# Rotary embedding kernel: half of unit 2 loaded as fp32 over ScalarE's queue, half of unit 3 stored by GpSimd

## Chip, cores and metric

One core of one Trainium2 chip. The metric is device microseconds of one execution; lower is better. "Span" is the time from the first to the last record of the profile. A DMA is one transfer between the chip's main memory (HBM) and the core's own (SBUF); a cast changes the number type, here between fp32 and fp16.

## The reference

The input `x` is (8, 8, 1024, 64) fp32, 16.8 MB, and the output is as large. For every position the two halves of the last dimension are rotated by an angle:

```python
angles = np.outer(positions * scale, freqs)          # (1024, 32)
cos, sin = np.cos(angles), np.sin(angles)
out_first  = x_first * cos - x_second * sin
out_second = x_first * sin + x_second * cos
```

## The kernel before

The 64 heads are cut in four "units" of 4 MB, each a tile of 128 partitions by N = 8192 elements (half: NH = 4096). GpSimd loads most of the data and lets the DMA cast it from fp32 to fp16; the second half of unit 0 alone comes as fp32 in two quarters over SyncE's and ScalarE's queues, and ScalarE casts it. VectorE rotates in fp16, ScalarE casts each half to fp32, and the result is stored. (`pin` keeps an instruction at its place in the program's order; lines are left out at `...` and at comments.)

```python
X0f = xout.tile([P, N], FP32, tag="O")               # staging, shares a slot with the outputs
Q = NH // 2
pin(nc.sync.dma_start(out=X0f[:, :Q], in_=xv[0][:, NH : NH + Q]))
pin(nc.scalar.dma_start(out=pos_i64, ...)); pin(nc.scalar.dma_start(out=freq_row, ...))
pin(nc.scalar.dma_start(out=X0f[:, Q:NH], in_=xv[0][:, NH + Q :]))
pin(nc.gpsimd.dma_start(out=Xf[0][:, :NH], in_=xv[0][:, :NH]))       # casts on the way
# ... small constants ...
for u in range(1, NU):
    c = C2 if u == NU - 1 else 0                     # unit 3 in two pieces
    pin(nc.gpsimd.dma_start(out=Xf[u][:, : N - c], in_=xv[u][:, : N - c]))
    if c:
        pin(nc.gpsimd.dma_start(out=Xf[u][:, N - c :], in_=xv[u][:, N - c :]))
# ... sine and cosine tables: VectorE, ScalarE, TensorE ...
pin(nc.scalar.copy(out=Xf[0][:, NH:], in_=X0f[:, :NH]))
for u in range(NU):
    OUT = xout.tile([P, N], FP32, tag="O")           # three slots
    for s in range(2):
        # ... pr = Xs*sin; Xs = Xs*cos; subtract; add (VectorE, fp16) ...
        pin(nc.scalar.copy(out=OUT[:, ns], in_=Xf[u][:, ns]))
        if u in (0, NU - 1):
            pin(nc.sync.dma_start(out=ov[u][:, ns], in_=OUT[:, ns]))
    if u not in (0, NU - 1):
        pin(nc.gpsimd.dma_start(out=ov[u], in_=OUT))
```

## Time and profile before

| | before |
|---|---|
| time, median of the 6 runs beside the change | 84.39 us |
| span of the profiled execution | 82.4 us |
| VectorE / ScalarE busy | 60.3 / 40.1 us |
| 16 DMA engines busy, three queues together | 80.2 us |
| first and last DMA packet | 1.75 and 81.15 us |
| last store landed | 81.5 us |

"Packet" is here one row of one partition, as the records of the trace have it; spread evenly, each of the 16 engines has 8 of the 128 rows of a DMA. The packets' times sum to more than the 79.4 us between first and last, as some packets of an engine overlap in the records: the sum measures work, not elapsed time. The first packet starts 1.75 us after the span's start and the last ends at 81.15; the DMA engines fill the time between.

### The profile page before, as it was taken

To read this page: it belongs to the slowest core of one execution; us is meant where nothing else is said; L and a number is where in the kernel's file an instruction comes from. 1 tells how busy PE (TensorE), PEld (TensorE's weight loads), DVE (VectorE), ACT (ScalarE), POOL (GpSimd) and SP (SyncE) were. 2 spreads that over 40 slices of the span, in tenths; PEclk is the share of its full clock that TensorE was granted. 3 is DMA by queue.
4 is the path that set the end of the run, shared out by engine and by line. 5 is a ranking of instruction groups with operands and counts; after the bars stand their busy time and mean duration, and the time that the engine had idled before them with its cause. 6 is when DMAs were issued, how large, how long until landed. Compare 5 with 4: busy or idle time off the path is not lost.

```text
span 82.4 us, 183 instructions
## 1 busy us (share of the span) xinstructions
PE 6.0 (7%) x18; PEld 2.4 (3%) x18; DVE 60.3 (73%) x40; ACT 40.1 (49%) x18; POOL 5.1 (6%) x15
## 2 busy tenths in 40 slices
PE   0011797100000000000000000000000000000000
PEld 0011232000000000000000000000000000000000
DVE  0306277999999999999999999999999998000000
ACT  0602259999950690294088049309705911950000
POOL 4950000000000000000000200000110000000000
PEclk9999999995555555555555555555555555555555
DMA  2899997996996999899899899997995998989992
GB/s 44 345 312 286 282 350 167 255 255 143 239 255 127 255 255 334 302 308 280 239 322 266 239 398 330 545 430 334 509 509 255 509 509 350 414 382 469 422 414 95
DMA packets 2018, 26.22 MB, mean 318 GB/s; under 512 B 354, under 2 KB 354, under 8 KB 482
## 3 DMA queue, kind: packets, MB, share of 16 engines
q0 software_dynamic: 1008, 15.73, 66.5%
q1 hardware_dynamic: 720, 9.44, 27.5%
q10 hardware_dynamic: 290, 1.06, 3.3%
HBM read 16.79 MB, written 16.78 MB: 407 GB/s over the span
## 4 chain that ended last, share of the span: by engine, by line
DVE 54%; ACT 15%; issue 7%; DMA 6%; PE 5%; DVEq 1%; ACTq 0%
DVE X L157 20%; DVE pr L156 20%; DVE X L161 9%; DMA freq_row<-in_freqs_dram 6%; ACT T L143 5%; DVE X L158 5%; ACT OUT L164 4%; ACT X L144 4%; PE ps L133 4%; DVEq L197 1%; PE cfreq L101 1%; ACT tab L126 1%; DVE r L117 1%; DVE y L108 1%; ACTq L70 0%
## 5 line engine op out<-in xcount | busy, mean ns | idle before, releaser
L164 ACT CAST OUT<-X 128x4096 f32<-128x4096 f16 x8 | 28.8, 3606 | 24.2 <-DVE X L161 24.2
L156 DVE TENSOR_TENSOR pr<-X,T 128x4096 f16<-128x4096 f16 x8 | 18.3, 2292 | 0.8 <-ACT T L143 0.5
L157 DVE TENSOR_TENSOR X<-X,T 128x4096 f16<-128x4096 f16 x8 | 18.3, 2292 | 0.3
L158 DVE TENSOR_TENSOR X<-X,pr 128x2048 f16<-128x2048 f16 x8 | 9.8, 1224 | 0.3
L161 DVE TENSOR_TENSOR X<-pr,X 128x2048 f16<-128x2048 f16 x8 | 9.7, 1217 | 0.0
L143 ACT CAST T<-ps 128x1024 f16<-128x1024 f32 x6 | 5.7, 1030 | 2.4 <-PE ps L133 2.4
L133 PE MATMUL ps<-tab,sel 128*128 128x512 f16 x16 | 5.4, 489 | 2.8 <-ACT tab L126 2.2
L168 POOL DMA_DIRECT2D out_dram<-OUT x2 | 1.1, 537 | 53.7 <-ACT OUT L164 53.7
L141 DVE CAST T<-ps 128x1024 f16<-128x1024 f32 x2 | 2.4, 1224 | 2.2 <-PE ps L133 2.2
L144 ACT CAST X<-X0f 128x4096 f16<-128x4096 f32 x1 | 3.6, 3650 | 0.0
L99 DVE COPY sel<-one 128x2048 f16<-128x2048 f16 x1 | 0.7, 693 | 2.8 <-POOL one L88 2.8
L121 ACT ACTIVATE tab<-r 128x256 f16<-128x256 f32 x1 | 0.4, 416 | 4.4 <-DVE r L117 4.4
L121 ACT ACT_TABLE_LOAD x1 | 1.3, 1283 | 2.1 <-issue 2.1
L133 PEld LDWEIGHTS <-sel 128*128 128x128 f16 x16 | 1.9, 120 | 5.9 <-issue 5.3
L94 POOL DMA_DIRECT2D X<-in_x_dram x3 | 2.0, 659 | 0.0
L104 DVE CAST posf<-pos_i 128x8 f32<-128x8 int32 x1 | 0.2, 171 | 2.1 <-DMA pos_i<-in_positions_dram 2.1
L101 PE MATMUL cfreq<-freq_row,coef 1*128 1x32 f32 x2 | 0.6, 392 | 5.9 <-DMA freq_row<-in_freqs_dram 5.9
L108 DVE TENSOR_TENSOR y<-posf,cfreq 128x256 f32<-128x256 f32 x1 | 0.4, 423 | 0.7 <-PE cfreq L101 0.7
L84 POOL DMA_DIRECT2D X<-in_x_dram x1 | 0.7, 667 | 0.8 <-POOLq L183 0.8
L101 PEld LDWEIGHTS cfreq<-freq_row,coef 1*128 1x128 f32 x2 | 0.5, 306 | 5.9 <-issue 5.9
L96 POOL DMA_DIRECT2D X<-in_x_dram x1 | 0.6, 558 | 0.0
L126 ACT ACTIVATE tab<-ra,quarter 128x256 f16<-128x256 f32 x1 | 0.5, 507 | 0.0
(11 smaller groups left out, 2.3 us busy)
## 6 DMA issues: line engine op xcount, KB each, us to landing
out_dram<-OUT SPq DMA_DIRECT2D x4, 2048.0 KB, 14.2
out_dram<-OUT POOLq DMA_DIRECT2D x2, 4096.0 KB, 14.8
X<-in_x_dram POOLq DMA_DIRECT2D x2, 2048.0 KB, 25.7
X<-in_x_dram POOLq DMA_DIRECT2D x1, 1792.0 KB, 44.6
X0f<-in_x_dram SPq DMA_DIRECT2D x1, 1024.0 KB, 4.7
X<-in_x_dram POOLq DMA_DIRECT2D x1, 1024.0 KB, 11.5
X0f<-in_x_dram ACTq DMA_DIRECT2D x1, 1024.0 KB, 13.4
X<-in_x_dram POOLq DMA_DIRECT2D x1, 256.0 KB, 47.7
```

Of the source, the lines that this page charges most:

```text
L94: pin(nc.gpsimd.dma_start(out=Xf[u][:, : N - c], in_=xv[u][:, : N - c]))
L101: nc.tensor.matmul(out=cfreq, lhsT=coef, rhs=freq_row, start=True, stop=True)
L121: pin(nc.scalar.activation(out=tab[:, 0], in_=r, func=AF.Sin, bias=0.0, scale=-_TWO_PI_DN))
L133: nc.tensor.matmul(out=ps[:, i].rearrange("p t w -> p (t w)"), lhsT=sel[:, g + i].rearrange("s h q -> s (h q)"), rhs=tab.rearrange("s t k ...
L141: pin(nc.vector.tensor_copy(out=dst, in_=ps))
L143: pin(nc.scalar.copy(out=dst, in_=ps))
L144: pin(nc.scalar.copy(out=Xf[0][:, NH:], in_=X0f[:, :NH]))
L156: pin(nc.vector.tensor_tensor(out=pr, in0=Xs, in1=sin_b, op=ALU.mult))
L157: pin(nc.vector.tensor_tensor(out=Xs, in0=Xs, in1=cos_b, op=ALU.mult))
L158: pin(nc.vector.tensor_tensor(out=Xs[:, :, 0, :], in0=Xs[:, :, 0, :], in1=pr[:, :, 1, :], op=ALU.subtract))
L161: pin(nc.vector.tensor_tensor(out=Xs[:, :, 1, :], in0=pr[:, :, 0, :], in1=Xs[:, :, 1, :], op=ALU.add))
L164: pin(nc.scalar.copy(out=OUT[:, ns], in_=Xf[u][:, ns]))
```

## The change

The intent, as far as the diff tells it: relieve GpSimd's queue of a sixth of its later loads (2 of 12 MB), use ScalarE's idle time for the cast, and let GpSimd share the last stores.

```diff
+    UF = 2
     pin(nc.scalar.dma_start(out=X0f[:, Q:NH], in_=xv[0][:, NH + Q :]))
+    pin(nc.scalar.dma_start(out=X0f[:, NH:], in_=xv[UF][:, NH:]))
...
     for u in range(1, NU):
         c = C2 if u == NU - 1 else 0
+        if u == UF:
+            pin(nc.gpsimd.dma_start(out=Xf[u][:, :NH], in_=xv[u][:, :NH]))
+            continue
...
             pin(nc.scalar.copy(out=OUT[:, ns], in_=Xf[u][:, ns]))
+            if (u, s) == (0, 1):
+                pin(nc.scalar.copy(out=Xf[UF][:, NH:], in_=X0f[:, NH:]))
             if u in (0, NU - 1):
-                pin(nc.sync.dma_start(out=ov[u][:, ns], in_=OUT[:, ns]))
+                eng = nc.gpsimd if (u, s) == (NU - 1, 0) else nc.sync
+                pin(eng.dma_start(out=ov[u][:, ns], in_=OUT[:, ns]))
```

## The prediction

> **What bounds the kernel now.** I began with the page's busy shares, because they name the obvious suspect, and then its table of DMA queues.
>
> ```profile
> PE 6.0 (7%) x18; PEld 2.4 (3%) x18; DVE 60.3 (73%) x40; ACT 40.1 (49%) x18; POOL 5.1 (6%) x15
> q0 software_dynamic: 1008, 15.73, 66.5%
> q1 hardware_dynamic: 720, 9.44, 27.5%
> q10 hardware_dynamic: 290, 1.06, 3.3%
> HBM read 16.79 MB, written 16.78 MB: 407 GB/s over the span
> ```
>
> VectorE is busy for 73% of the span, but the three DMA queues together take 66.5 + 27.5 + 3.3 = 97.3% of the time of the 16 DMA engines, that is 80.2 of 82.4 us. q0 is GpSimd's queue, q1 SyncE's, q10 ScalarE's. (q0's 15.73 MB count the bytes written; its loads read fp32 and write fp16, so 7.34 MB of loads stand for 14.68 MB read, beside 8.39 MB of stores.) Next I asked for the DMA share in stretches that leave out the first 2 us, before the first packet, and the last, after it.
>
> ```profile
> 2.00:12.00 10.00, 3.86 (x11) 1.79 (x12) 4.03 (x8) 3.20 (x4) 3.12 (x8) 1.00 1.00 303
> 12.00:22.00 10.00, 2.16 (x9) 0.62 (x7) 9.31 (x6) 9.86 (x7) 0.00 (x0) 0.83 1.07 230
> 22.00:32.00 10.00, 0.00 (x0) 0.00 (x0) 9.86 (x6) 5.44 (x2) 0.00 (x0) 0.50 0.97 220
> 62.00:72.00 10.00, 0.00 (x0) 0.00 (x0) 7.54 (x5) 5.93 (x2) 0.00 (x0) 0.50 0.96 415
> 2.00:81.50 79.50, 6.02 (x18) 2.41 (x18) 60.30 (x40) 40.13 (x18) 4.20 (x10) 0.60 1.00 329
> ```
>
> The column before the last is the DMA share: 1.00 from 2.0 to 81.5 us. (Rows stray between 0.9 and 1.07 because a packet is credited where it starts. Cutting the packet records into 1 us bins, I find 1.00 to 1.07 of the engines busy in every bin between the first and the last.) The DMA engines never rest, so bytes set the end. The other candidate is VectorE and the tail behind it: half of the chain of waits (54%) is VectorE. From the timeline (start, duration), and the landing time of the store issued from 73 to 74 us:
>
> ```profile
> 13.19 2.29 DVE L156 TENSOR_TENSOR pr<-X,T 128x4096 f16<-128x4096 f16 x1 [0.47 <-ACT T L143]
> ...
> 27.39 2.29 DVE L156 TENSOR_TENSOR pr<-X,T 128x4096 f16<-128x4096 f16 x1
> 27.45 3.60 ACT L164 CAST OUT<-X 128x4096 f32<-128x4096 f16 x1 [3.61 <-DVE X L161]
> ...
> 69.67 3.60 ACT L164 CAST OUT<-X 128x4096 f32<-128x4096 f16 x1 [3.39 <-DVE X L161]
> ```
>
> ```profile
> out_dram<-OUT SPq DMA_DIRECT2D x1, 2048.0 KB, 8.2
> ```
>
> VectorE runs without a gap from 13.19 to 69.65 us. ScalarE's last cast ends at 73.27, and the last 2 MB store, issued there, lands 8.2 us later, at 81.5. By itself it would be faster: SyncE's first load started about 1.25 us after its issue, and 8 rows per engine of 16 KB at 0.611 us take 4.9 us, so VectorE's chain alone would let the end come at about 73.3 + 1.25 + 4.9 + 0.2 = 79.7. It lands at 81.5 because unit 2's store holds the engines until about 72 and the first half of unit 3 goes before it. VectorE thus has about 1.8 us to spare at the last store.
>
> **What the Trainium skill says.** "DMA: Bandwidth & Descriptors", section "Issuing engines are not separate DMA queues": transfers started by different engines run on the same 16 DMA engines and interleave. The 97.3% sum agrees. The same page, "Queues, rings and completion order", says that each engine takes turns among the queues by packet. The trace agrees: when GpSimd's load of unit 2 and SyncE's store of unit 0 overlap, 28 to 34 us, each queue passes 48 packets. The same page, "SWDGE vs HWDGE vs iDMA", says that only GpSimd's DMAs can cast, which is why the moved load needs a ScalarE cast. "ScalarE: Activation LUTs", section "What ACT_TABLE_LOAD costs", gives 186 ns + 0.833 ns per element with immediate operands: 3598 ns for 4096; the trace has 3606 and 3650.
>
> **The change part by part.**
>
> *The moved load.* 2 MB of unit 2 leave q0, where a row of 16 KB fp32 became 8 KB fp16, and enter q10, where it stays fp32. HBM bytes do not change. DMA time: in the packet records a cast packet from 16 KB takes 0.624 us and one from 32 KB 1.227 us; a plain packet of 16 KB takes 0.611 to 0.624 (stores) and one of 8 KB 0.307 to 0.322. That is 26.3 to 26.8 GB/s per engine in every kind. 128 packets times at most 0.013 us, over 16 engines, is 0.1 us. The cast in the DMA was free, so taking it out gains nothing.
>
> *The new cast.* One ScalarE cast of 128x4096 fp32 to fp16, 3.65 us as in this row:
>
> ```profile
> L164 ACT CAST OUT<-X 128x4096 f32<-128x4096 f16 x8 | 28.8, 3606 | 24.2 <-DVE X L161 24.2
> L144 ACT CAST X<-X0f 128x4096 f16<-128x4096 f32 x1 | 3.6, 3650 | 0.0
> ```
>
> It stands in order behind the OUT cast of unit 0's second half, which runs 27.45 to 31.05, so it runs 31.05 to 34.70. The next OUT cast started at 34.44: 0.26 us late, with 3.4 us of idle time behind it (the 24.2 us over seven waits). It delays no VectorE work.
>
> *Where the order of arrival moves.* This is the one sensitive spot. The moved load queues behind unit 0's quarter and starts at about 12.5, when unit 0's transfers end. From then q10 takes turns with q0's load of unit 1, which had the engines to itself and landed at 22.5 (issued about 2.7, 19.8 to land). Per engine there are 8 packets of 1.227 us and now 8 of about 0.62 between them: it lands about 8 x 0.62 = 5.0 us later, at about 27.5. VectorE wants unit 1 at 27.39. SyncE's store of unit 0, issued at 23.86, does not push it further: before, its first packet started at 28.7, about 1.25 us of issue and three packets already in the engines after its issue. So VectorE stalls by 0 to 0.6 us, I take 0.2. ScalarE gets its fp32 at about 28, before 31.05. Unit 2's first half then needs only 2 MB from q0 and lands near 37 (8 packets each of q0 and q1, 9.8 us after 27.5), wanted at 41.49; unit 3 lands near 51, wanted at 55.58. No other load is late.
>
> *The store.* Half 0 of unit 3 goes to q0, in line behind unit 2's 4 MB, instead of q1. Before, it was issued at 66.3 and its first packet came near 71, as unit 2's ended: it already ran where it would on q0. The other half, issued at 73.3, found it still running until 76.6. On two queues they might alternate, but the same 4 MB leave at the same rate, 16 x 0.611 = 9.8 us from 72. GpSimd's issue costs 0.54 us on an idle engine. Sum: 0.
>
> *Buffers.* The staging tile shares its slot with unit 2's output; ScalarE first writes that at 48.53, and the new reader ends at 34.70. No wait.
>
> Sum: the DMA work changes by at most 0.1 us and VectorE shifts by about 0.2, out of a slack of 1.8 us at the last store and of about 1 to 1.5 us at unit 2's store (issued 59.48, wanted by the engines at 62.1, less 1 to 1.5 us that a GpSimd DMA may take to start). I put 84.4 us.
>
> **Rivals.** *A late unit 1 is felt.* If the engines favour q10, or its load is served ahead of q0, unit 1 could land at 29 to 30, and VectorE stalls 2 to 2.5 us. Then unit 2's store starts late while nothing else is in any queue, the engines rest 1 to 1.5 us, and the end moves to 85.5 to 86. For it: the 27.5 against 27.39 has no margin. Against it: turns by packet gave equal counts in the trace, and q10's rows are half as long as q0's. *The cast in the DMA has a cost that I miss*, and moving it and spreading the last store speeds up the end. For it: that is the likely intent. Against it: packet times per byte are equal, and the engines have no idle time to win; 33.56 MB in the 79.4 us from first to last packet are already 423 GB/s, at 26.8 per engine the most would be 428, so at best 1.1 us: 83.3. *ScalarE becomes the bound.* It goes from 40.1 to 43.8 us of 82; the row above shows 3.4 us of idle before each cast, so no.
>
> **Range and chances.** Runs of one kernel spread by 0.3 us. The downside is the stall, the upside half a microsecond of better interleaving: 83.8 to 85.5. Faster by 2% would need 82.7, under what the bytes allow: 0.02. Slower by 2% needs 86.05, a stall near 3 us: 0.06. Same: 0.92.
>
> **What would show it.** The DMA share over 2 to 81.5 stays 1.00 and the three shares still sum to about 80 us. q10 grows by 2.1 MB to 3.2 and by about 5 us of engine time, 6% of the span, to 9.4%; q1 falls to 7.34 MB and 21.5%; q0 loses 1.05 MB of load and gains 2.10 of store, for 16.78 MB at an unchanged 66.5%. The row of the staging cast becomes x2 at about 3650 ns. The pr row of VectorE waits at most 0.6 us for unit 1's load. The last store still lands near 81.5. I am wrong if a wait of VectorE for that load exceeds 1.5 us and the engines show a gap after 62, or if a fp32 packet of 16 KB takes clearly other than 0.62 us.

## The result and the profile after

84.90 us median of 6 runs (84.72 to 85.11) beside 84.39 of before; ratio 1.0063, interval 1.0041 to 1.0085. Ratios here are the mean time of one kernel's runs over the mean of the other's of the same rounds, so they are not quite the ratio of the medians quoted. The change is "same" at 2%, and slower by a small amount that is clear of the noise. The page after has the busy shares and queues as foreseen:

```profile
PE 6.9 (8%) x18; PEld 2.7 (3%) x18; DVE 60.3 (73%) x40; ACT 43.7 (53%) x19; POOL 5.7 (7%) x16
q0 software_dynamic: 1152, 16.78, 65.8%
q1 hardware_dynamic: 576, 7.34, 21.5%
q10 hardware_dynamic: 434, 3.15, 9.9%
HBM read 16.79 MB, written 16.78 MB: 406 GB/s over the span
```

The queues now sum to 97.2% of 82.7 us, 80.4 us of engine time; the HBM bytes are the same to the last digit shown. In the stretches of the span the engines again rest nowhere (DMA share before the last column):

```profile
22.00:32.00 10.00, 0.00 (x0) 0.00 (x0) 9.11 (x6) 6.39 (x3) 0.00 (x0) 0.50 0.99 281
2.00:81.50 79.50, 6.95 (x18) 2.70 (x18) 60.31 (x40) 43.65 (x19) 4.74 (x11) 0.60 1.01 342
```

The timeline shows the one new wait of VectorE, and the new cast:

```profile
27.32 3.61 ACT L170 CAST OUT<-X 128x4096 f32<-128x4096 f16 x1 [3.61 <-DVE X L167]
28.02 2.29 DVE L162 TENSOR_TENSOR pr<-X,T 128x4096 f16<-128x4096 f16 x1 [0.79 <-DMA X<-in_x_dram]
...
30.83 3.60 ACT L172 CAST X<-X0f 128x4096 f16<-128x4096 f32 x1
...
35.07 3.61 ACT L170 CAST OUT<-X 128x4096 f32<-128x4096 f16 x1 [0.64 <-DVE X L167]
```

The page's rows of the two staging casts, and the landing of the last store (issued between 73 and 75 us):

```profile
L149 ACT CAST X<-X0f 128x4096 f16<-128x4096 f32 x1 | 3.6, 3648 | 0.0
L172 ACT CAST X<-X0f 128x4096 f16<-128x4096 f32 x1 | 3.6, 3599 | 0.0
```

```profile
out_dram<-OUT SPq DMA_DIRECT2D x1, 2048.0 KB, 7.8
```

The new cast is as long as the old one, and the last store, issued at 74.00, lands at 81.8: issued 0.7 us later than before, it lands only 0.3 later. VectorE waits 0.79 us for unit 1, which shared the engines with the moved load. Everything on VectorE is from there on some 0.7 us later, yet the last DMA packet ends at 81.42 instead of 81.15. ScalarE's cast fits in its gap: the next output cast starts when VectorE is ready.

A trap stands in the chain of waits: it now runs through this load,

```profile
DVE 45%; DMA 30%; issue 6%; ACT 4%; DVEq 1%; POOL 1%; POOLq 0%
```

and gives "DMA 30%" to it. One could read that the load of unit 1 has become the bound. The chain follows who released whom; it cannot see that the last store waited in the engines behind other stores, so its percentages do not say what a shorter wait is worth.

One more number comes from the list of runs: time minus span, per run. Before: 1.77 us (median of the 40 runs beside the experiments). After: 2.06 (median of 6). So of the 0.5 us, about 0.25 lie inside the span (median 82.6 against 82.85) and about 0.3 outside it, where the profile shows nothing.

### The profile page after: what moved, and what is told of

It is laid out like the page before. It is cut to its first block, busy times and chain, and to the rows that moved or that the text cites. A ratio compares the mean times of both kernels' runs of the same rounds, so it can differ in the third digit from the quotient of the medians.

```text
span 82.7 us, 186 instructions
## 1 busy us (share of the span) xinstructions
PE 6.9 (8%) x18; PEld 2.7 (3%) x18; DVE 60.3 (73%) x40; ACT 43.7 (53%) x19; POOL 5.7 (7%) x16
## 3 DMA queue, kind: packets, MB, share of 16 engines
q0 software_dynamic: 1152, 16.78, 65.8%
q1 hardware_dynamic: 576, 7.34, 21.5%
HBM read 16.79 MB, written 16.78 MB: 406 GB/s over the span
## 4 chain that ended last, share of the span: by engine, by line
DVE 45%; DMA 30%; issue 6%; ACT 4%; DVEq 1%; POOL 1%; POOLq 0%
DMA X<-in_x_dram 30%; DVE pr L162 17%; DVE X L163 17%; DVE X L167 7%; DVE X L164 5%; ACT OUT L170 4%; DVEq L206 1%; POOL one L90 0%; POOL coef L87 0%; POOL one L89 0%; POOL X L86 0%; DVEq L162 0%; POOL quarter L88 0%; POOLq L192 0%
## 5 line engine op out<-in xcount | busy, mean ns | idle before, releaser
L170 ACT CAST OUT<-X 128x4096 f32<-128x4096 f16 x8 | 28.9, 3607 | 21.5 <-DVE X L167 21.5
L138 PE MATMUL ps<-tab,sel 128*128 128x512 f16 x16 | 6.3, 582 | 2.2 <-ACT tab L131 2.2
L177 POOL DMA_DIRECT2D out_dram<-OUT x2 | 1.1, 538 | 54.4 <-ACT OUT L170 54.4
L149 ACT CAST X<-X0f 128x4096 f16<-128x4096 f32 x1 | 3.6, 3648 | 0.0
L172 ACT CAST X<-X0f 128x4096 f16<-128x4096 f32 x1 | 3.6, 3599 | 0.0
L99 POOL DMA_DIRECT2D X<-in_x_dram x2 | 1.4, 720 | 0.0
L175 POOL DMA_DIRECT2D out_dram<-OUT x1 | 0.5, 533 | 6.5 <-ACT OUT L170 6.5
L86 POOL DMA_DIRECT2D X<-in_x_dram x1 | 0.7, 669 | 0.8 <-POOLq L192 0.8
```

What stands on the lines that cost most here:

```text
L138: nc.tensor.matmul(out=ps[:, i].rearrange("p t w -> p (t w)"), lhsT=sel[:, g + i].rearrange("s h q -> s (h q)"), rhs=tab.rearrange("s t k ...
L172: pin(nc.scalar.copy(out=Xf[UF][:, NH:], in_=X0f[:, NH:]))
```

## Experiments

**The two parts alone, and the load elsewhere.** The edits, against the change (e1, e3, e4) or against before (e2):

```diff
# e1_load_only: the change without its store
-                eng = nc.gpsimd if (u, s) == (NU - 1, 0) else nc.sync
-                pin(eng.dma_start(out=ov[u][:, ns], in_=OUT[:, ns]))
+                pin(nc.sync.dma_start(out=ov[u][:, ns], in_=OUT[:, ns]))
# e2_store_only: before with the change's store
# e3_fp32_on_q0: e1, with the load on GpSimd's queue and the cast one step later
-    pin(nc.scalar.dma_start(out=X0f[:, NH:], in_=xv[UF][:, NH:]))
+            pin(nc.gpsimd.dma_start(out=X0f[:, NH:], in_=xv[UF][:, NH:]))   # behind unit 2's first half
-            if (u, s) == (0, 1):
+            if (u, s) == (1, 0):
# e4_load_late: e1, with the load still on ScalarE's queue, issued behind unit 0's cast; cast as in e3
```

> The load and its cast alone; the last stores as before. Theory 'load' (the fp32 load shares the engines with unit 1's load and its packets take longer: 0.24 us more engine time in the changed kernel): 84.8 to 84.9 us, with the 0.7 us wait of VectorE for unit 1. Rival 'store' (GpSimd's store costs the time): 84.4 us.

> The store on GpSimd's queue alone. Theory 'load': 84.4 us, engine time 80.1 us, last landing as before. Rival 'store': 84.9 us.

> Unit 2's second half still comes as fp32 and is cast by ScalarE (one step later), but over GpSimd's queue behind unit 2's first half, so that nothing is added beside unit 1's load; stores as before. If fp32 against cast in the DMA matters by itself: 84.7 to 84.9, or under 84.2 if the cast had a cost. If only the place in the order matters: 84.4 us, no wait of VectorE for unit 1.

> The fp32 load stays on ScalarE's queue, but is issued behind the cast of unit 0's quarters (about 20 us), so that it meets unit 2's first half and SyncE's store and not unit 1. Unit 1 lands by 24, VectorE waits for nothing. If VectorE's 0.7 us wait is what the 0.5 us are: 84.4. If the meeting of three queues lengthens packets whatever they carry: 84.7 to 84.9 without any wait.

| | DMAs (on SyncE's and ScalarE's queues) | time us | ratio to before | span us | time minus span | VectorE's wait for unit 1 |
|---|---|---|---|---|---|---|
| before | 15 (8) | 84.39 | | 82.6 | 1.77 | none |
| after | 16 (8) | 84.90 | 1.0063 | 82.85 | 2.06 | 0.8 |
| e1 load only | 16 (9) | 85.26 | 1.0105 | 83.2 | 2.06 | 0.5 |
| e2 store only | 15 (7) | 84.37 | 1.0001 | 82.6 | 1.77 | none |
| e3 fp32 on q0 | 16 (8) | 84.81 | 1.0048 | 82.75 | 2.04 | none |
| e4 load late | 16 (9) | 85.37 | 1.0113 | 83.3 | 2.07 | none |

Times and spans are medians over the runs of a kernel (before: the time in the rounds of e1 to e4, the other two over all 40 runs). The store alone is free. The load costs something wherever it is put, with VectorE's wait or without: e4 has none for a load and is the slowest. (In e3 the profile puts a wait of 0.8 us ahead of unit 0 and 6.4 us of idle ScalarE down to a store that keeps a buffer; its time is still just that of the change.) So the wait is not what costs. By its expectation e3 speaks for fp32 against the cast in the DMA; that reading fails with e9 below. Two things were not expected. First, e1 and e4 are slower than the change itself, by 0.36 and 0.47 us: the store of the change gives time back, though alone it is worth nothing. Second, time minus span takes only two values, 1.8 and 2.05, and goes with 15 or 16 DMAs.

The first was found in SyncE's records at the end, read from the trace itself and not from a view. SyncE waits there for the semaphores of all DMAs (a semaphore is a counter that a finished DMA raises), one after the other. Starts of these waits after the last store's issue, with us from the span's start (last store landed at 81.49, 81.76 and 81.90):

```
before  73.69 73.75 73.82 73.88 73.94 74.00 74.06 76.66 81.51 | drain 81.57
after   76.95 77.02 77.09 77.15 77.21 77.27 77.33 77.39 81.78 | drain 81.84
e1      74.46 81.91 81.97 82.04 82.10 82.16 82.22 82.28 82.34 | drain 82.41
```

The DMAs on SyncE's and ScalarE's queues share eight semaphores. With eight such DMAs or fewer the last store has the last place that SyncE looks at; the ninth in e1 and e4 comes back to the first semaphore, so that SyncE walks seven more waits of 0.06 us after the data have landed: 82.41 - 81.90 = 0.51 us from landing to drain, instead of 0.08. The profile shows the same as one long wait in place of two, first the change and then e1:

```profile
SPq L206 <- DMA out_dram<-OUT: 6.9, 2, 4.3
```

```profile
SPq L205 <- DMA out_dram<-OUT: 7.4, 1, 7.4
```

By handing one store to GpSimd the change keeps the number at eight. That is what its store part is worth: about 0.4 us, but only beside the load part. e4's records show the same seven waits after its last landing (starts from 82.16 to 82.53).

**Sixteen DMAs, or the cast, or fp32?** e9, e10 and e11 start from before:

```diff
# e9_split_cast: unit 2 in two halves on GpSimd's queue, both cast by the DMA (16 DMAs)
-        c = C2 if u == NU - 1 else 0
+        c = C2 if u == NU - 1 else NH if u == 2 else 0
# e10_extra_cast: one more ScalarE cast, into a scratch tile, where the change has its own (15 DMAs)
+            if (u, s) == (0, 1):
+                pin(nc.scalar.copy(out=scratch, in_=X0f[:, :NH]))
# e11_fewer_dmas: unit 3 loaded by one DMA, unit 0 stored by one (13 DMAs)
-        c = C2 if u == NU - 1 else 0
+        c = 0
...                                                   # and unit 0's output is stored whole, behind its second half, over SyncE
```

> The kernel before with unit 2 loaded in two halves by GpSimd, both cast in the DMA: one DMA more (16 instead of 15), no fp32 half, no ScalarE cast. So far every kernel with the moved load has 16 DMAs and one more ScalarE instruction, and its time exceeds its span by 2.0 to 2.1 us instead of 1.8. Theory 'number of DMAs': excess 2.05 and 84.65 us or more. Rival 'fp32 or ScalarE instruction': excess 1.8 and 84.4.

> The kernel before plus one ScalarE cast of 128x4096 fp32 into a scratch tile nobody reads, at the place of the change's cast. 15 DMAs. Theory 'number of DMAs': 84.4 us, excess over the span 1.8. Rival 'the cast costs': 84.65 or more.

> The kernel before with unit 3 loaded by one DMA instead of two and unit 0 stored by one instead of two: 13 DMAs, the same bytes. Theory 'number of DMAs' (0.28 us each outside the span): excess 1.2 to 1.5 us and 83.8 to 84.1 us, faster than both. Rival: 84.4.

e9: 84.89 us, ratio 1.0049 (1.0025 to 1.0073), time minus span 2.05, span 82.8. Its unit 2 has neither an fp32 half nor a ScalarE cast nor a load on another queue, and it costs the same half microsecond as the change. e10: 84.52 us, ratio 1.0021 with an interval from 0.998 to 1.006, and time minus span 1.77. That interval, widened by one run of 85.44, would by itself not exclude a cost of the cast; but e9 has the full cost without the cast. So what the change adds outside the span goes with the sixteenth DMA, not with the cast or fp32; e9's span of 82.8 has the rest, of which more below. e11 was a miss: time minus span stayed at 1.8 with 13 DMAs, so, as far as 13, 15 and 16 tell, it is a step between 15 and 16 and not a price per DMA; and its six runs fell in two groups, three at 84.3 and three at 85.2 to 85.3. In its profile, of the second group, the records end at 82.22 though the engines' packets sum to less than before (79.9 us). All packets but two end by 81.11, as before, and those two at 81.61 and 82.22, so one engine or two ended late; why is not known.

**Is it the DMA engines that set the end?** e7 and e8 start from before and give wrong results on purpose:

```diff
# e7_no_subtract
+            if u == 0:
                 pin(nc.vector.tensor_tensor(... op=ALU.subtract))
# e8_half_stores
-            pin(nc.gpsimd.dma_start(out=ov[u], in_=OUT))
+            pin(nc.gpsimd.dma_start(out=ov[u][:, :NH], in_=OUT[:, :NH]))
```

> The kernel before without the subtract in units 1 to 3, wrong on purpose: VectorE has 6 x 1.2 = 7 us less to do, the bytes are the same. Theory 'the DMA engines are the bound': 84.2 to 84.4 us, last packet at 81.2 to 81.4. Rival 'VectorE's chain is the bound': about 77.5.

> The kernel before with only half of the outputs of units 1 and 2 stored, wrong on purpose: 4 MB, 9.8 us of the DMA engines' time, fall away and VectorE is untouched. If the engines set the end and VectorE's tail is 1.7 us behind: 82.5 to 82.7 us, with engines idle before the last store. If VectorE's chain were the bound all along: 84.3.

e7: 84.36 us, ratio 0.9994. VectorE did 6.8 us less, and the time did not move:

```profile
2.00:81.50 79.50, 5.92 (x18) 2.35 (x18) 53.49 (x34) 40.13 (x18) 4.19 (x10) 0.60 1.00 329
```

e8: 82.10 us, ratio 0.9745, somewhat under the 82.5 to 82.7 expected. With 9.8 us of DMA work taken away only 2.2 us came off; the engines now rest while VectorE works, and the last packet ends at 78.94, 5.9 us after the last store's issue at 73.04:

```profile
62.00:66.00 4.00, 0.00 (x0) 0.00 (x0) 3.93 (x3) 3.59 (x1) 0.00 (x0) 0.50 0.00 0
```

The two together say where the kernel stands: the DMA engines are the bound and VectorE's chain is 2.2 us behind.

**How much waiting is free?** e5 and e6 delay unit 1 by loading unit 2, in part or whole, ahead of it:

```diff
# e5_unit1_3mb_late; e6_unit1_4mb_late has E = 8192 and skips unit 2 in the loop
+    E = 6144
+    pin(nc.gpsimd.dma_start(out=Xf[2][:, :E], in_=xv[2][:, :E]))
     for u in range(1, NU):
...                                                   # the loop loads the rest of unit 2
```

> The kernel before with 3 MB of unit 2 loaded ahead of unit 1 on GpSimd's queue: unit 1 lands near 29.8 and VectorE waits about 2.4 us instead of 0.7; one DMA more. Theory 'VectorE has slack until the engines would idle at unit 2's store' (its issue at 61.9, first packet 1.4 us later, engines free at 62.0): they rest about 1.2 us, and the end moves by 1.2 plus the 0.3 of a DMA more: 85.7 to 86.0. Rival 'any stall is paid in full': 86.8 to 87.1. Rival 'stalls are free': 84.4 to 84.7.

> The kernel before with units 1 and 2 in reverse order on GpSimd's queue (4 MB ahead): unit 1 lands near 32.3, VectorE waits about 4.9 us, 15 DMAs. Slack theory: the engines rest about 3.8 us, 88.3 us. In full: 89.3. Free: 84.4.

Both waits came out longer than expected, because SyncE's store of unit 0, whose first packet came at 28.55 and 28.67 us, now arrived during unit 1's load and took turns with it (the load's last packet: 31.4 and 34.5):

```profile
DVE pr L159 <- DMA X<-in_x_dram: 5.1, 1, 5.1
```

```profile
DVE pr L159 <- DMA X<-in_x_dram: 8.1, 1, 8.1
```

e5 took 88.66 us, e6 91.39, beside 84.27 in the same rounds. e5 has 16 DMAs: less 0.3 its wait of 5.1 us cost 4.1; e6's wait of 8.1 cost 7.1. Both leave 1.0 us free and pay the rest in full, which neither "free" nor "in full" would give. The packet records say the same: in e5 and e6 unit 2's store has its first packet 1.10 us after its issue, on idle engines; before, issued at 59.48, it could have begun at 60.6 and began at 61.46, so 0.9 us were to spare. The times that I had put down were about 2.7 and 3.1 us too low, as the waits were mis-sized, but the form of the slack theory holds. In e5 the engines stand still from 62.5 to 65.6 us, before unit 2's store, as it foresaw:

```profile
62.00:66.00 4.00, 0.00 (x0) 0.00 (x0) 3.93 (x3) 2.23 (x1) 0.53 (x1) 0.50 0.31 131
```

The change's wait of 0.79 us is under 1.0 us, so it cost nothing.

**The change with 15 DMAs.** One edit to the changed kernel: unit 3 by one DMA (`c = 0`).

> The changed kernel with unit 3 loaded by one DMA instead of two: 15 DMAs again, eight of them on SyncE's and ScalarE's queues, the fp32 half, the cast and GpSimd's store all kept. If the sixteenth DMA is what takes the time outside the span: excess over the span 1.8 and 84.6 us (the span stays at 82.8 for the split rows). Rival, the fp32 load on ScalarE's queue does: excess 2.05 and 84.9 us. Unit 3 as one DMA can make the time jump by 1 us in some runs, as it may have with the 13 DMAs.

84.55 us, ratio 1.001 (0.9986 to 1.0034), time minus span 1.75, span 82.8. With load, cast and store all kept, the part outside the span is gone. (The jump of 1 us, seen in e11 and feared here, came in none of the six runs.) No correct kernel tried is clearly faster than before. The best a rearrangement could do is small, by an estimate from the best packet times of before, on 16 engines: 16.79 MB of loads at 427 GB/s (32 KB in 1.227 us) and 16.78 MB of stores at 432 GB/s (32 KB in 1.213 us) take 78.1 us, and they take 79.4.

## Why the prediction was right

The prediction gave 84.4 us, 83.8 to 85.5, "same" at 0.92; measured 84.90. Its mechanism held: the engines set the end, and the late unit 1 stayed within the slack. One term was mis-sized and two were missing. That the store kept the sum at 0.5 us was luck as far as the prediction goes: without it the same load took 0.9 (e1).

- *The DMA engines are the bound.* Right, and shown by e7 and e8. Its estimate of VectorE's slack at the last store, 1.8 us, is 2.2 by e8. It gave a SyncE DMA 1.25 us from issue to first packet; the first load took 1.01 (0.74 to 1.75), and e8's last stores, on idle engines, 0.84. Its bins of 1.00 to 1.07 I recount as 0.94 (the first, a part of it idle) to 1.13; the reading stands.
- *Moving the load does not change DMA time.* Right about fp32 against cast: e9, with casts alone, costs what the change costs. Mis-sized at 0.1 us: I compared packets of equal size, wrote "26.3 to 26.8 GB/s per engine in every kind", where plain 8 KB rows at 0.322 us have 25.4 and 32 KB stores at 1.213 us 27.0, and overlooked that the split turns rows of 32 KB into two of 16 KB, in both halves. The moved fp32 rows took 0.624 us each (median), as foreseen. A 32 KB cast row takes 1.227 us, two 16 KB rows 0.624 each: 8 rows per engine x (1.248 - 1.227) = 0.17 us. The engine time rose by 0.24 us, the last packet came 0.27 later in the profiled runs, the median span grew by 0.25. The two profiles cannot carry this: before's is of its fastest run (84.16 us), and those of e2 and e10, with unit 2's rows whole, have 80.3 and 80.7 us of engine time, beside 80.1 before and 80.4 after. The median spans fit the rows (e9, e3, e12: 82.8, 82.75, 82.8, beside 82.5 to 82.6 of before), but e10's is 82.75 too, with runs from 82.4 to 83.7. So the 0.17 us are an estimate from packet times; that they are most of the span's 0.25 is not shown.
- *Missing: the sixteenth DMA.* About 0.28 us outside the span. Every kernel with 16 DMAs shows 2.04 to 2.07 us of time over span (six kernels), every one with 15 or 13 shows 1.75 to 1.80 (eight); e9 puts it in and e12 takes it out. It is not the number of semaphores: e1 uses no more of them than before, 15, and has it. What happens there, and whether it is the DMA itself or something that comes with it, is open; no record of the profile covers it. This and the span's 0.25 make the 0.5 us that were measured.
- *Unit 1 lands at about 27.5, VectorE stalls by 0 to 0.6 us.* It landed at 27.93 and VectorE stalled 0.79. A little long, and within the slack. The prediction put the slack at unit 2's store at 1 to 1.5 us; e5 and e6 measure 1.0, so the margin left was small. It read the first packet of unit 0's store at 28.7 us, where the records have 28.45; nothing hangs on it.
- *The new cast delays nothing.* Right; 3.60 us at 30.83. The 0.26 us foreseen for the next output cast did not come, as VectorE was later than that. e10 shows no clear cost.
- *The store: sum 0.* Right alone (e2). Missing: that it keeps the last store's semaphore last in SyncE's list and so spares the change 0.4 us (e1 against the change).
- *The queues after.* q1 as foreseen, 7.34 MB and 21.5%; q0 16.78 MB and 65.8 instead of 66.5%; q10 9.9 instead of 9.4%.
- *Rivals.* The late unit 1 was late but not felt. A hidden cost of the cast in the DMA does not show. (The most that the bytes allow is 1.3 us by the estimate above, not 1.1.) ScalarE did not become the bound.

## What to carry to other kernels

With the DMA engines busy from the first packet to the last, moving a load to another queue, and its cast to an idle engine, won nothing here: add up packet time and compare it with the time between first and last packet before looking at engines. A wait that a profile newly shows, even one at the head of the chain that ended last, cost only what exceeded the slack behind it; delaying the same load further measures that slack. And at half a microsecond, count DMAs: one more cost time in two places, about 0.4 us in the order in which the last semaphores are waited for (the ninth on SyncE's and ScalarE's queues) and about 0.3 outside the span (the sixteenth of all).

## What the Trainium skill lacked or had wrong

- "DMA: Bandwidth & Descriptors" and "Runtime: NRT & Kernel Launch" have no step with the number of DMAs: time over span was 1.8 us with 13 or 15 and 2.05 with 16.
- No page has the order of the last waits: SyncE's seven further semaphore waits after the last landing took 0.43 us in e1.
- "DMA: Bandwidth & Descriptors", section "Where 436 GB/s comes from", says that about 358 GB/s bind for transfers between HBM and SBUF. Read alone, that is too low for one core: here loads and stores together ran at 423 GB/s (33.56 MB in 79.4 us). The page's own section "Bandwidth" gives about 358 for both cores streaming, and "Perfetto Trace Analysis", section "Roofline", allows a single core more than that share; both agree with the 423.
- The same page, section "Queues, rings and completion order", gives turns by packet but not how long a newcomer waits: SyncE's store, issued at 23.86 us while GpSimd's 32 KB rows were in service, had its first packet at 28.45, where e8's last stores, on idle engines, had theirs 0.84 us after issue: a wait of some 3.7 us more, or three rows of 1.227 us.
